# A hybrid decoder layer: thirteen shared up-projection blocks instead of ten, and more weight buffers for the feed-forward

## The chip, the cores and the metric

The kernel runs on one core of a Trainium2 chip. The metric is the device time of one execution in microseconds. A profile of one execution gives the time of each instruction on the engines: TensorE (PE, matmuls; PEld, its weight loads), VectorE (DVE), ScalarE (ACT), GpSimd (POOL), and the queue from which SyncE (SP) issues the transfers (DMA).

## What is computed

One layer on a sequence of 1024 tokens of 1024 channels, all in float32. The mixer and the feed-forward each have a norm before and after; what matters here is the feed-forward with its 2 x 2816 up columns, a causal convolution of width 3 along the tokens on each column, a gated product, and the down projection.

```python
def _conv_ffn(h, ffn_up, ffn_conv_w, ffn_conv_b, ffn_down):
    hid = h @ ffn_up.astype(h.dtype)
    hid = _causal_dwconv(hid, ffn_conv_w, ffn_conv_b)
    gate, up = hid[..., :D_FF], hid[..., D_FF:]
    return (jax.nn.gelu(gate, approximate=True) * up) @ ffn_down.astype(h.dtype)

def reference(...):
    ...
        h = _rms_norm(x, norm_pre_mix[i])
        mix, v_first = _hybrid_mixer(h, ...)
        x = x + _rms_norm(mix, norm_post_mix[i])
        h = _rms_norm(x, norm_pre_ffn[i])
        f = _conv_ffn(h, ffn_up[i], ffn_conv_w[i], ffn_conv_b[i], ffn_down[i])
        x = x + _rms_norm(f, norm_post_ffn[i])
```

The mixer before it has a recurrence over the tokens for 8 heads (in chunks of 64 tokens), a convolution of width 31 over 512 channels, and an output projection.

## The kernel before

**Products in three passes.** A float32 operand is split into a rounded part `hi` and a rest `lo` (`split`: ScalarE writes `hi`, GpSimd or VectorE subtracts to get `lo`). A product is the sum of hi x hi, hi x lo and lo x hi, three matmuls of a 128 x 128 weight with 512 tokens. A weight of 128 x 512 is loaded into a raw buffer (tag `wr`), split into a pair (tags `wh`, `wl`), and used by four input tiles, so by 12 matmuls. In the kernel before, there are 3 raw buffers and 2 pairs, in the pool `wp`.

**Tokens in two halves.** The sequence is worked on in two halves of 512 tokens, `h0` and `h1` for the feed-forward's normed input, each 8 tiles of 128 channels. The up projection has 22 blocks; block i has a gate of 128 columns and an up part of 128 columns.

**Plain blocks.** `ffn_pair(h, hs, i, ...)` computes block i for one half: two products over 8 tiles (48 matmuls), the taps of the convolution (`taps`), gelu and the product. Blocks 0 to 11 (`EARLY` = 12) are computed for the first half inside the mixer, with a low priority, so that TensorE has work while VectorE and the recurrence set the pace there; their results go to memory (`early`) and come back before the down projection. Blocks 0 to `PLAIN` - 1 = 11 are computed for the second half after the mixer, and also go to memory (`plain`).

**Shared blocks.** The last `JOINT` = 10 blocks are computed for both halves together. Gate and up columns, the two halves of the tokens, and the two halves of the 1024 channels make a product of 2 x 2 by 2 x 2 blocks; with sums of the operands it takes seven block products instead of eight (12 matmuls each). `gates` computes two of the seven with the first half alone, while the second half is normed: 24 matmuls a block, the results kept in two tiles per block of the pool `actp` (2 x `JOINT` tiles of 2 KB per partition). `act_sums` forms the sums of the activations (S), a step at a time beside the plain blocks. `shared` computes the other five: it loads the four raw weights of the block (`raws`), forms their sums on GpSimd (`four_sums`, four instructions), splits five weights, and does 60 matmuls, five additions on VectorE, and the taps of both halves. The first shared block takes sums that were formed before (`usums`).

**Side work.** `weight_sums` forms sums of down-projection weights (eleven steps, and one for the first shared block): four loads, four GpSimd instructions (L1056), four stores each. `beside` runs a step of side work between blocks: in `gates` the second half's norm first, and then norm and sums in every other block; in the plain blocks a step of sums in each, and one or two of `act_sums`.

**The down projection.** `ffn_down` is again seven products instead of eight, with 924 matmuls; it uses all 22 blocks of both halves.

**Order.** The order on each engine is set when the program is built, by a planner that simulates the engines with its own costs and takes instructions by priority as their buffers and inputs come free. `high_priority` puts loads and splits of weights ahead. All transfers are issued from SP's queue in the planned order. Buffers of a tag are reused in turn; an instruction that writes a buffer waits for the last reader.

In the mixer's end, `w_out(1, ...)`, the output projection of the second half, follows the early blocks in the same stream "proj". Its weights pass through `wr` into the buffers "ca" and "ck" of the recurrence, and its inputs are splits of `mixr` (recurrence, finished at L760) and `co` (convolution) into tiles "l8".

Of the kernel before, what the change touches and what calls it, by code (L numbers as in the profile page):

```python
# [22 lines left out]
P = 128  # L23
# [26 lines left out]
BUFS = {"v": 2, "gd": 1, "pt": 6, "kk": 1, "l8": 5, "ca": 6, "ck": 6, "r": 2,  # L50
        "mixr": 1, "co": 4, "po": 1, "c": 4, "t2": 2}

EARLY = 12

JOINT = 10
PLAIN = FT - JOINT

PRIO = {"first": -1000, "top": 100000, "rwkv": 1000, "norm": 200000, "conv": 300000, "proj": 400000}

# [39 lines left out]
class Trunk:  # L99
    def __init__(self, ctx, tc, a):  # L100
# [3 lines left out]

        self.low_pool = True


    def nm(self, s):
        self.n += 1
# [49 lines left out]
    def split(self, hi, lo, src, pool=False):  # L159

        eng = self.nc.gpsimd if pool else self.nc.vector
        return self.nc.scalar.copy(hi, src), eng.tensor_tensor(lo, src, hi.bitcast(F32), ALU.subtract)  # L162

    def weight(self, src, shape, home=None, held=None, kept=None):


        with self.tc.high_priority():
            raw = (self.f2p.tile(shape, F32, tag="f2", name=self.nm("wr")) if held is self.hp else
                   self.wp.tile(shape, F32, tag="wr", bufs=3, name=self.nm("wr")))
            self.load = self.nc.sync.dma_start(raw, src)  # L170
            if held:
                hi, lo = self.pair("w", held)
            elif home:
                hi, lo = (home[0].tile(shape, F32R, tag=t, bufs=BUFS[t], name=self.nm("wm")) for t in home[1:])
            else:
                hi, lo = (self.wp.tile(shape, F32R, tag=t, bufs=2, name=self.nm(t)) for t in ("wh", "wl"))
            if kept and kept[0]:
                self.nc.scalar.copy(hi, raw)  # L178
                self.nc.sync.dma_start(lo.bitcast(F32), kept[1])
            else:  # L180
                self.low = self.split(hi, lo, raw, self.low_pool)[1]
        if kept and not kept[0]:
            self.nc.sync.dma_start(kept[1], lo.bitcast(F32))
        return hi, lo


    def setup(self):
        nc, tc, ctx, a = self.nc, self.tc, self.ctx, self.a
        pool = lambda name, **kw: ctx.enter_context(tc.tile_pool(name=name, bufs=1, **kw))
        self.cp = pool("const")  # L190
        self.small = ctx.enter_context(tc.tile_pool(name="small", bufs=4))
        self.wp = ctx.enter_context(tc.tile_pool(name="wp", bufs=1))
        self.hp = ctx.enter_context(tc.tile_pool(name="hp", bufs=2 * KT))
        self.dp = pool("dram", space=DRAM)
        self.rowp = pool("rowp")
        self.psum = pool("psum", space=PSUM)
        cp = self.cp
        self.params = cp.tile([P, NPAR], F32, name="params")
        self.const = cp.tile([P, NCONST], F32, name="const")
        with self.stream("first"):  # L200
            nc.sync.dma_start(self.const[:, :P], a["consts"][:, :P])
        nc.sync.dma_start(self.params, a["params"])
        nc.sync.dma_start(self.const[:, P:], a["consts"][:, P:])
        self.mhalf = cp.tile([P, 8], F32, name="mhalf")
        nc.gpsimd.memset(self.mhalf, -0.5)
        self.mixd = self.dp.tile([SEQ, D], F32, name="mixd")
        self.early = self.dp.tile([EARLY, P, HALF], F32, name="early")
        self.x1d = self.dp.tile([SEQ, D], F32, name="x1d")
        self.ssq = cp.tile([P, 8, 4], F32, name="ssq")
        self.lows = self.dp.tile([22, 2, P, 4, P], F32, name="lows")  # L210
        self.sums = self.dp.tile([4, HT, P, 512], F32, name="sums")
        self.plain = self.dp.tile([PLAIN, P, HALF], F32, name="plain")
        self.usums = self.dp.tile([4, P, 512], F32, name="usums")
        self.ecarry = cp.tile([P, 2, EARLY, 2], F32, name="ecarry")

    def setup_mixer(self, ctx):
        nc, tc, a = self.nc, self.tc, self.a
        pool = lambda name, bufs=1: ctx.enter_context(tc.tile_pool(name=name, bufs=bufs))
        cp = pool("mconst")
        self.mix = pool("mix")  # L220
        self.banks = {"pb": 2, "pc": 1, "pe": 2}
        self.xs = [self.psum.tile([P, 512], F32, name=f"xs{g}") for g in range(2)]
        self.wa = cp.tile([P, HALF], F32, name="wa")

        self.dw = cp.tile([P, 16 + 1024], F32, name="dw")
        nc.gpsimd.memset(self.dw[0:64, 528:1040], 0.0)
        self.Y = self.psum.tile([P, 512], F32, name="Y")


        self.lora = cp.tile([G_LORA, D_RWKV], F32, name="lora")
        nc.sync.dma_start(self.lora, a["lora"][:G_LORA, 2])
        self.lw = cp.tile([96, 2, D_RWKV], F32R, name="lw")
        for e in range(2):
            raw = self.wp.tile([P, D_RWKV], F32, tag="wr", bufs=3, name=self.nm("wr"))
            nc.sync.dma_start(raw, a["lora"][:, e])
            nc.scalar.copy(self.lw[:, e], raw[0:96])
            low = self.lw[64:96, e]
            nc.gpsimd.tensor_tensor(low, raw[64:96], low.bitcast(F32), ALU.subtract)  # L240
        self.lx = cp.tile([96, 2, QUARTER], F32R, name="lx")
        n = POFF["k_k"]
        self.omu = cp.tile([P, n], F32, name="omu")
        nc.vector.tensor_scalar(self.omu, self.params[:, :n], -1.0, 1.0, ALU.mult, ALU.add)

        self.hw0 = cp.tile([P, 8], F32, name="hw0")
        nc.vector.tensor_scalar(self.hw0, self.params[:, POFF["w0"]:POFF["w0"] + 8], 0.5, None, ALU.mult)
        self.ka = cp.tile([P, 8], F32, name="ka")
        ka = self.params[:, POFF["k_a"]:POFF["k_a"] + 4]
        nc.vector.tensor_scalar(self.ka[:, 0:4], ka, 0.5, None, ALU.mult)  # L250
        nc.vector.tensor_scalar(self.ka[:, 4:8], ka, -0.5, 1.0, ALU.mult, ALU.add)
        cw = self.params[:, POFF["cw"]:POFF["cw"] + 4 * CONV_W]
        nc.vector.tensor_scalar(cw, cw, 0.5, None, ALU.mult)
        self.carry = cp.tile([P, n], F32, name="carry")
        self.ccarry = cp.tile([P, 4, 32], F32, name="ccarry")[:, :, :CONV_W - 1]
# [561 lines left out]
    def setup_ffn(self, ctx):  # L817
        nc, tc = self.nc, self.tc
        pool = lambda name, bufs=1: ctx.enter_context(tc.tile_pool(name=name, bufs=bufs))
        cp = pool("fconst")  # L820

        self.turn = cycle([lambda: self.xs[0], lambda: self.xs[1]]
                          + [lambda t=t: Trunk.bank(self, t) for t in ("pe", "pe", "pb", "pb")])
        self.bank = lambda tag="pb": self.Y if tag == "pn2" else Trunk.bank(self, "pc") if tag == "pn" else next(self.turn)()
        self.nrowp = pool("nrowp")

        self.ap = pool("actp", 2 * JOINT)
        self.h1p = pool("h1p", 2 * KT)
        self.tp = pool("tp", 8)
        self.f2p = pool("f2p", 6)  # L830
        self.post_ffn = cp.tile([P, D], F32, name="post_ffn")
        nc.sync.dma_start(self.post_ffn, self.a["post_ffn"].broadcast_to([P, D]))
        self.fcarry = cp.tile([P, 2, 32, 2], F32, name="fcarry")
        self.fss = cp.tile([P, 8, 48], F32, name="fss")
# [169 lines left out]
    def shared(self, i, S, A22, act0, act1, raws):  # L1004
# [10 lines left out]
        if raws is None:  # L1015
            T = lambda n: self.weight(kview(self.usums[n - 1]), [P, 4, P])
            b22 = lambda: self.weight(up[FT + i, 1], [P, 4, P])
        else:
            with self.tc.high_priority():
                b11, b12, b21, b22r = raws  # L1020
                for n in (1, 3, 0, 2):
                    self.load = nc.sync.dma_start(kview(raws[n]), up[n % 2 * FT + i, n // 2])
                t3 = self.wp.tile([P, HALF], F32, tag="wr", bufs=3, name=self.nm("t3"))
                self.four_sums(b11, b12, b21, b22r, t3)

            def pair(raw):
                with self.tc.high_priority():
                    hi, lo = (self.wp.tile([P, HALF], F32R, tag=t, bufs=2, name=self.nm(t)) for t in ("wh", "wl"))
                    self.low = self.split(hi, lo, raw, True)[1]
                return kview(hi), kview(lo)  # L1030

            T = lambda n: pair((b12, b11, t3, b21)[n - 1])
            b22 = lambda: pair(b22r)
# [167 lines left out]
    def run(self):  # L1201
# [6 lines left out]
        with ExitStack() as ctx:  # L1208
# [24 lines left out]
            for i in range(0, 8, 2):  # L1233
                two = self.row("row", 4)
                nc.sync.dma_start(two.rearrange("p (i t) -> p i t", i=2), self.early[i:i + 2].rearrange("i p t -> p i t"))
                kept += [two[:, :HALF], two[:, HALF:]]
            back = [self.hp.tile([P, HALF], F32, tag="h", name=self.nm("act")) for _ in range(2 * KT)]
            for i in range(8, EARLY):
                nc.sync.dma_start(back[PLAIN + i - 8], self.early[i])
            for i in range(PLAIN):  # L1240
# [220 lines left out]

# [6 lines left out]
```

## Time and profile before

| | |
|---|---|
| median of 3 runs | 1274.57 us (1273.83 to 1277.31) |
| profiled execution | 1273.13 us, its span 1271.4 us |
| TensorE busy | 1220.3 us (96%), 8460 matmuls |
| VectorE, ScalarE, GpSimd busy | 891.2, 731.1, 495.4 us |
| early blocks' first matmul | 497.7 us |
| second output projection, first matmul | 668.1 us |
| gates' first matmul | 698.8 us |
| plain blocks, shared blocks, down projection begin | 776.5, 911.0, 1051.9 us |

A row of the groups gives line, engine, operation, output <- inputs (buffer numbers left out), shapes and count; then busy time and mean duration in ns; then the engine's idle time before these instructions and what ended it. A row of the chain, which follows the work that ended last back to the beginning, gives start, length, engine, output and line, and the count. A row of the stages gives busy time and number of instructions of each engine in a stretch, then the granted clock of TensorE, the share of the DMA engines and GB/s. Durations of matmuls overlap. `f` are the feed-forward's inputs, `s` their sums, `wh` and `wl` a split weight; `pb`, `pe`, `pc`, `xs`, `Y` are banks of PSUM.

### The profile page before, as it was taken

To read this page: it belongs to the slowest core of one execution; us is meant where nothing else is said; L and a number is where in the kernel's file an instruction comes from. 1 tells how busy PE (TensorE), PEld (TensorE's weight loads), DVE (VectorE), ACT (ScalarE), POOL (GpSimd) and SP (SyncE) were. 2 spreads that over 40 slices of the span, in tenths; PEclk is the share of its full clock that TensorE was granted. 3 is DMA by queue.
4 is the path that set the end of the run, shared out by engine and by line. 5 is a ranking of instruction groups with operands and counts; after the bars stand their busy time and mean duration, and the time that the engine had idled before them with its cause. 6 is when DMAs were issued, how large, how long until landed. Compare 5 with 4: busy or idle time off the path is not lost.

```text
span 1271.4 us, 23025 instructions
## 1 busy us (share of the span) xinstructions
PE 1220.3 (96%) x8460; PEld 990.1 (78%) x8460; DVE 891.2 (70%) x1540; ACT 731.1 (58%) x1518; POOL 495.4 (39%) x438
## 2 busy tenths in 40 slices
PE   6999989999999988999999999999999999999996
PEld 4767767787778877788789878778877888888885
DVE  5286998998679989997631165666356779479667
ACT  7563563655845766566744277776555556545451
POOL 4343320011113332344455369898588860000001
PEclk9999998999999999999999999999999999999999
DMA  7644342343343451232345398888522236336523
GB/s 242 173 133 141 117 134 75 94 134 124 110 135 86 122 183 66 85 84 84 101 132 166 112 336 299 292 305 268 173 65 73 79 127 222 99 98 194 173 76 133
DMA packets 105505, 185.70 MB, mean 146 GB/s; under 512 B 15184, under 2 KB 21712, under 8 KB 105392
## 3 DMA queue, kind: packets, MB, share of 16 engines
q1 hardware_dynamic: 105392, 184.23, 46.2%
q8 instruction: 67, 1.10, 0.4%
q14 instruction: 46, 0.38, 0.1%
HBM read 141.58 MB, written 42.60 MB: 145 GB/s over the span
## 4 chain that ended last, share of the span: by engine, by line
PE 55%; DVE 8%; DMA 3%; POOL 3%; issue 2%; ACT 2%; SPq 0%; POOLq 0%; DVEq 0%; ACTq 0%
PE pb L135 26%; PE pe L135 13%; PE xs L135 11%; PE Y L135 2%; DVE pc L416 2%; PE pc L135 2%; POOL wl L162 1%; DVE nrow L1116 1%; DVE x L1100 1%; POOL b L1056 1%; PE pc L150 1%; DMA pt<-mixd 1%; DMA m<-mixd 1%; PE pe L150 0%; DMA b<-ffn_down 0%
## 5 line engine op out<-in xcount | busy, mean ns | idle before, releaser
L162 POOL TENSOR_TENSOR wl<-wr,wh 128x512 fp32r<-128x512 f32 (+1 forms) x181 | 237.2, 1312 | 247.7 <-ACT wh L162 221.0
L162 ACT CAST wh<-wr 128x512 fp32r<-128x512 f32 (+1 forms) x220 | 135.5, 616 | 170.7 <-issue 43.9
L135 PE MATMUL pb<-h,wh 128*128 128x512 f32 (+3 forms) x720 | 229.5, 398 | 2.5 <-ACT wh L162 1.0
L135 PE MATMUL pb<-f,wh 128*128 128x512 f32 x696 | 219.0, 395 | 2.6 <-ACT wh L162 1.5
L416 DVE SCALAR_TENSOR_TENSOR pc<-c,params,pc 128x512 f32<-128x512 f32 x232 | 174.1, 750 | 8.8 <-ACT pc L413 4.8
L135 PEld LDWEIGHTS pb<-h,wh 128*128 128x128 f32 (+2 forms) x720 | 131.8, 188 | 34.9 <-ACT wh L162 2.6
L135 PEld LDWEIGHTS pb<-f,wh 128*128 128x128 f32 x696 | 130.0, 189 | 31.0 <-ACT wh L162 2.8
L135 PE MATMUL pb<-h,wl 128*128 128x512 f32 (+3 forms) x360 | 146.4, 407 | 2.3 <-POOL wl L162 2.1
L135 PE MATMUL pb<-f,wl 128*128 128x512 f32 x348 | 137.9, 397 | 1.5 <-POOL wl L162 1.5
L157 POOL TENSOR_TENSOR ss<-var,mhalf 128x1 f32<-128x1 f32 x16 | 11.0, 692 | 222.6 <-DVE ss L1097 198.2
L1056 POOL TENSOR_TENSOR b<-b,b 128x512 f32<-128x512 f32 x66 | 86.8, 1317 | 2.8 <-issue 0.9
L135 PE MATMUL pe<-f,wh 128*128 128x512 f32 x272 | 84.2, 391 | 0.1
L135 PEld LDWEIGHTS pb<-h,wl 128*128 128x128 f32 (+2 forms) x360 | 67.7, 188 | 20.7 <-POOL wl L162 4.5
L135 PEld LDWEIGHTS pb<-f,wl 128*128 128x128 f32 x348 | 65.7, 189 | 16.9 <-POOL wl L162 3.1
L135 PE MATMUL xs<-f,wh 128*128 128x512 f32 x200 | 62.0, 391 | 0.4 <-DVE act L953 0.4
L135 PEld LDWEIGHTS pe<-f,wh 128*128 128x128 f32 x272 | 50.9, 188 | 10.6 <-ACT wh L162 0.3
L899 DVE SCALAR_TENSOR_TENSOR pt<-pb,params,pt 128x511 f32<-128x511 f32 (+1 forms) x48 | 35.7, 743 | 30.0 <-ACT ecarry L892 29.5
L162 POOL TENSOR_TENSOR wl<-b,wh 128x512 fp32r<-128x512 f32 x36 | 47.0, 1307 | 21.7 <-ACT wh L162 19.8
L135 PE MATMUL pe<-f,wl 128*128 128x512 f32 x136 | 53.7, 395 | 0.7 <-POOL wl L162 0.7
L706 POOL TENSOR_TENSOR XG<-r,GE 64x256 f32<-64x256 f32 x30 | 20.4, 683 | 86.9 <-DVE r L725 82.0
L178 ACT CAST wh<-wr 128x512 fp32r<-128x512 f32 (+2 forms) x44 | 26.5, 604 | 43.1 <-PE pb L135 31.2
L162 ACT CAST wh<-b 128x512 fp32r<-128x512 f32 x36 | 22.2, 617 | 46.8 <-PE pb L135 18.9
(428 smaller groups left out, 2883.7 us busy)
## 6 DMA issues: line engine op xcount, KB each, us to landing
wr<-ffn_up SPq DMA_DIRECT2D x117, 256.0 KB, 2.8
wr<-w_in SPq DMA_DIRECT2D x80, 256.0 KB, 2.9
b<-ffn_down SPq DMA_DIRECT2D x44, 256.0 KB, 4.4
sums<-b SPq DMA_DIRECT2D x44, 256.0 KB, 4.0
wr<-sums SPq DMA_DIRECT2D x44, 256.0 KB, 2.7
lows<-wl SPq DMA_DIRECT2D x40, 256.0 KB, 3.3
wl<-lows SPq DMA_DIRECT2D x40, 256.0 KB, 2.7
b<-ffn_up SPq DMA_DIRECT2D x40, 256.0 KB, 2.7
```

The source lines that it names most:

```text
L135: return self.nc.tensor.matmul(out, lhsT, rhs, start=start, stop=stop, skip_group_check=skip)
L150: self.nc.tensor.transpose(out, in_, self.con("ident")[:n, :n])
L157: self.nc.gpsimd.tensor_tensor(out, v[:, :n], self.mhalf[:, :n], ALU.pow)
L162: return self.nc.scalar.copy(hi, src), eng.tensor_tensor(lo, src, hi.bitcast(F32), ALU.subtract)
L178: self.nc.scalar.copy(hi, raw)
L416: nc.vector.scalar_tensor_tensor(out, c[:, j:j + HALF], w(j), acc, ALU.mult, ALU.add)
L706: nc.gpsimd.tensor_tensor(x[64:128], R[64:128, gs], w.GE[64:128, c, gs].unsqueeze(2).broadcast_to([64, 4, CH]), ALU.mult)
L899: nc.vector.scalar_tensor_tensor(acc[:, o:], ps[:, :HALF - o], w(j), acc[:, o:], ALU.mult, ALU.add)
L1056: sub = lambda o, x, y, op=ALU.subtract: self.nc.gpsimd.tensor_tensor(o, x, y, op)
L1100: nc.vector.scalar_tensor_tensor(x, f[c], s[:, 1:2], x, ALU.mult, ALU.add)
L1116: nc.vector.tensor_tensor(out, a, b, op)
```

## The change

`EARLY` becomes 9 and `JOINT` 13, so `PLAIN` becomes 9: three blocks that were plain in both halves become shared. The pool `actp` grows from 20 to 26 tiles. A new pool `wq` holds two raw buffers and one pair more; weights of the feed-forward take buffers of `wq` and `wp` in turn (`wtile`), those of the mixer stay with `wp`. The memory for DMA descriptors in SBUF is set to 1024 bytes, which frees the space. `ecarry` keeps its size. Fewer tiles are taken for the reload of early and plain results.

```diff
-EARLY = 12
-JOINT = 10
+EARLY = 9
+JOINT = 13
 PLAIN = FT - JOINT
+RAW, MORE_RAW, PAIRS, MORE_PAIRS = 3, 2, 2, 1
...
+        once = [None]
+        self.homes = {"wr": cycle(once), "wh": cycle(once), "wl": cycle(once)}
...
+    def wtile(self, tag, shape, dt=F32):
+        pool = next(self.homes[tag]) or self.wp
+        bufs = {self.wp: (RAW, PAIRS), self.wq: (MORE_RAW, MORE_PAIRS)}[pool][tag != "wr"]
+        return pool.tile(shape, dt, tag=tag, bufs=bufs, name=self.nm(tag))
...
     def weight(self, src, shape, home=None, held=None, kept=None):
...
-                   self.wp.tile(shape, F32, tag="wr", bufs=3, name=self.nm("wr")))
+                   self.wtile("wr", shape))
...
-                hi, lo = (self.wp.tile(shape, F32R, tag=t, bufs=2, name=self.nm(t)) for t in ("wh", "wl"))
+                hi, lo = (self.wtile(t, shape, F32R) for t in ("wh", "wl"))
...
+        self.wq = ctx.enter_context(tc.tile_pool(name="wq", bufs=1))
...
-        self.ecarry = cp.tile([P, 2, EARLY, 2], F32, name="ecarry")
+        self.ecarry = cp.tile([P, 2, 12, 2], F32, name="ecarry")
...
     def setup_ffn(self, ctx):
...
+        self.homes = {"wr": cycle([self.wq] * MORE_RAW + [self.wp] * RAW),
+                      **{t: cycle([self.wq] * MORE_PAIRS + [self.wp] * PAIRS) for t in ("wh", "wl")}}
...
     def shared(self, i, S, A22, act0, act1, raws):
...
-                t3 = self.wp.tile([P, HALF], F32, tag="wr", bufs=3, name=self.nm("t3"))
+                t3 = self.wtile("wr", [P, HALF])
...
-                    hi, lo = (self.wp.tile([P, HALF], F32R, tag=t, bufs=2, name=self.nm(t)) for t in ("wh", "wl"))
+                    hi, lo = (self.wtile(t, [P, HALF], F32R) for t in ("wh", "wl"))
...
-            back = [self.hp.tile([P, HALF], F32, tag="h", name=self.nm("act")) for _ in range(2 * KT)]
+            back = [self.hp.tile([P, HALF], F32, tag="h", name=self.nm("act")) for _ in range(PLAIN + EARLY - 8)]
...
-    nc = bacc.Bacc("TRN2", target_bir_lowering=False, num_devices=1)
+    nc = bacc.Bacc("TRN2", target_bir_lowering=False, num_devices=1, dynamic_dma_scratch_size=1024)
```

More of the change, by code (lines that the diff above doesn't have):

```diff
@@ L235, in setup_mixer @@
         for e in range(2):
-            raw = self.wp.tile([P, D_RWKV], F32, tag="wr", bufs=3, name=self.nm("wr"))
+            raw = self.wtile("wr", [P, D_RWKV])
             nc.sync.dma_start(raw, a["lora"][:, e])
```

## The prediction

> **What bounds the kernel now.** I read the page first (shares, slices, chain), then busy times by stage, then the chain in order of time, then what TensorE waits for in the feed-forward.
>
> ```profile
> span 1271.4 us, 23025 instructions
> PE 1220.3 (96%) x8460; PEld 990.1 (78%) x8460; DVE 891.2 (70%) x1540; ACT 731.1 (58%) x1518; POOL 495.4 (39%) x438
> PE   6999989999999988999999999999999999999996
> DVE  5286998998679989997631165666356779479667
> POOL 4343320011113332344455369898588860000001
> DMA  7644342343343451232345398888522236336523
> PE 55%; DVE 8%; DMA 3%; POOL 3%; issue 2%; ACT 2%; SPq 0%; POOLq 0%; DVEq 0%; ACTq 0%
> ```
>
> TensorE (PE) is busy 96% of the span and is the largest part of the chain; from slice 16 on it shows 9 up to the last. POOL is high in slices 23 to 32 only, DMA in slices 23 to 28 (counted from 0). So each stage behind about 500 us is as long as its matmuls, unless something feeds them late. What a matmul costs there is not its mean duration, since they overlap, but the length of an unbroken run:
>
> ```profile
> 850.57 5.44 PE pb L135 x24
> 986.16 10.90 PE pb L135 x48
> 1041.21 10.88 PE pb L135 x48
> ```
>
> 10.90 us for 48 is 0.227 us for one matmul of 512 columns. The stages:
>
> ```profile
> core 0: us, PE busy (x) PEld busy (x) DVE busy (x) ACT busy (x) POOL busy (x), PEclk, DMA share, GB/s
> 628.00:668.00 40.00, 37.95 (x166) 30.76 (x166) 15.86 (x23) 21.20 (x43) 20.56 (x16) 1.00 0.44 126
> 668.00:699.00 31.00, 31.00 (x259) 30.96 (x258) 5.61 (x7) 12.65 (x32) 16.52 (x14) 1.00 0.57 169
> 699.00:776.00 77.00, 74.70 (x396) 62.62 (x395) 35.70 (x63) 42.21 (x99) 43.32 (x36) 1.00 0.71 239
> 776.00:911.00 135.00, 133.55 (x582) 107.80 (x581) 75.03 (x111) 95.15 (x200) 110.57 (x88) 1.00 0.80 268
> 911.00:931.00 20.00, 18.35 (x77) 13.79 (x76) 10.97 (x16) 10.03 (x21) 17.32 (x14) 1.00 0.34 122
> 931.00:1052.00 121.00, 120.94 (x527) 97.52 (x526) 79.83 (x116) 67.91 (x141) 94.29 (x72) 1.00 0.33 98
> 1052.00:1060.00 8.00, 8.00 (x37) 6.63 (x36) 8.00 (x13) 4.59 (x11) 0.00 (x0) 1.00 1.05 386
> ```
>
> In order: the last early blocks; the second output projection alone; its rest with the gates of the ten shared blocks; the twelve plain blocks of the second half; the shared blocks (two rows); the first 8 us of the down projection.
>
> **The change, part by part.** A plain block costs 48 matmuls in each half. A shared block costs 24 in the gates and 60 (five products of 12) in the shared stage: 84 for both halves instead of 96. Three blocks change kind:
>
> - Early blocks in the mixer, 12 to 9: 3 x 48 = 144 matmuls fewer, 144 x 0.227 = -32.7 us.
> - Gates, 10 to 13: 3 x 24 = 72 more, +16.3 us.
> - Plain blocks of the second half, 12 to 9: 144 fewer, -32.7 us.
> - Shared stage, 10 to 13: 3 x 60 = 180 more, +40.9 us.
>
> The sum is 36 matmuls fewer, -8.2 us. With the stages' real lengths per block (135 / 12 = 11.25 us plain, 141 / 10 = 14.1 us shared, stalls and transposes included) it is -32.7 + 16.3 - 33.8 + 42.3 = -7.9 us.
>
> **Does the mixer give its 32.7 us back?** Only if those blocks are on the path there. One row of PE and two of VectorE (DVE) by time, a group of DVE from 632 to 674 us, and a row of the chain:
>
> ```profile
> 604.18 1.14 PE L135 MATMUL Y<-r,ca 128*64 128x64 f32 x16
> 622.52 0.69 DVE L760 TENSOR_TENSOR mixr<-mixr,pe 128x512 f32<-128x512 f32 x1
> 629.36 2.50 DVE L162 TENSOR_TENSOR l<-co,l 128x512 fp32r<-128x512 f32 x4 [0.56 <-ACT l L162]
> L912 DVE TENSOR_TENSOR row<-pt,pt 128x512 f32<-128x512 f32 x4 | 3.4, 856 | 0.1
> 633.05 46.72 PE pb L135 x250
> ```
>
> The mixer's own work ends with L760 at 623.2 us and the last split of the output projection's inputs at 631.9 us. After that four more early blocks end (x4), and PE runs without a break from 633.05 to the projection at 668. Three of these four blocks go. The projection then starts at 668.1 - 32.7 = 635.4 us, 3.5 us after its inputs are ready: the cover is thin but there. If the planner's order put those splits later, what is over 3.5 us would be lost. The projection's weights, also moved up by 32.7 us, need POOL for 16 splits: POOL is busy 20.56 of 40 us there, so half is free. Their buffers are those of the recurrence, which reads them last at 605.3 us (`Y<-r,ca`). I take the whole -32.7.
>
> **Other engines, per changed block.** Rows of the plain stage (776 to 911), of the shared stage (931 to 1050), and of the whole run:
>
> ```profile
> L162 POOL TENSOR_TENSOR wl<-wr,wh 128x512 fp32r<-128x512 f32 x49 | 63.3, 1293 | 21.9 <-ACT wh L162 21.4 <-DMA wr<-ffn_up 0.2 <-DMA usums<-b 0.2
> L1056 POOL TENSOR_TENSOR b<-b,b 128x512 f32<-128x512 f32 x39 | 50.5, 1294 | 1.9 <-issue 0.9
> L162 POOL TENSOR_TENSOR wl<-t,wh 128x512 fp32r<-128x512 f32 x9 | 13.5, 1505 | 1.2 <-ACT wh L162 1.2
> L1048 DVE TENSOR_TENSOR act<-act,acc 128x512 f32<-128x512 f32 x8 | 9.8, 1227 | 0.0
> L899 DVE SCALAR_TENSOR_TENSOR acc<-xs,params,acc 128x511 f32<-128x511 f32 (+1 forms) x16 | 11.2, 743 | 6.3 <-ACT fcarry L892 6.3
> L1116 DVE TENSOR_TENSOR act<-act,act 128x512 f32<-128x512 f32 x17 | 11.2, 680 | 0.0
> ```
>
> POOL does 8 splits (10.3 us) for a block that is plain twice, and 7 splits and 4 sums (14.3 us) for a shared one; DVE some 7.5 and 12 us (8 taps at 0.74, a copy, five additions and two products). So 12 us more on POOL and 14 on DVE, all in the shared stage, where PE needs 13.6 us per block, POOL 11.8 and DVE 79.83 / 121 = 66%. I cost them at nothing; PE's run covers them. ACT makes one cast fewer per block. DMA falls: two weight loads, two stores and two reloads fewer per block, 18 transfers of 256 KB in all. With them goes the work on SP's queue, and some of the burst of reloads at 1052 (386 GB/s), which stops nobody today.
>
> The plain stage gets tighter. The twelve sums of weights (eleven of the down projection, one of the up) are now spread over four side turns in thirteen gates and eight of nine plain blocks, before three and nine of twelve. A plain block with a sum takes POOL 4 x 1.293 + 4 x 1.294 = 10.4 us of the 10.9 that PE takes, and moves 13 x 262 KB = 3.4 MB, or 313 GB/s. Both hold today in nine blocks; the three blocks without a sum, in which they could catch up, shrink to one.
>
> **The buffers.** Raw weight buffers of the feed-forward go from 3 to 5, split pairs from 2 to 3. What they can win is bounded by PE's waits from 690 to 1050 us:
>
> ```profile
> PE pb L135 <- POOL wl L162: 1.0, 2, 0.7
> PE pb L135 <- ACT wh L162: 0.8, 2, 0.5
> PE pe L135 <- ACT wh L162: 0.8, 1, 0.8
> PE pe L135 <- POOL wl L162: 0.7, 1, 0.7
> PE xs L135 <- POOL wl L162: 0.7, 2, 0.3
> PE pc L150 <- ACT nrow L872: 0.4, 1, 0.4
> ```
>
> The five rows on weights (`wh`, `wl`) sum to 4.0 us; that is the most there is. A pair is 12 matmuls, 2.7 us of lookahead; a sum's four POOL instructions take 5.2, so a third pair should hide about half: I take -1.5 us, between 0 and -4. Against it stands the tighter plain stage: bounded by nothing, and by 8 blocks x 1 us (a block with a sum at 11.9 instead of 10.9), +8 us; I take 0, since the present nine such blocks cost less than the 4.0 us above. The smaller descriptor memory: the trace has one queue with data, filled from SP (q1, hardware_dynamic, below), and no transfer issued by POOL; I take nothing. The first feed-forward loads now have free buffers from the beginning, and could be issued far earlier, at worst among the loads of the first slices: two of 262 KB at the first slice's 242 GB/s are 2.2 us; I take 0, as the planner follows priorities.
>
> ```profile
> q1 hardware_dynamic: 105392, 184.23, 46.2%
> ```
>
> [...]
>
> From the rows alone: a shared block loses 1.23 - 0.68 = 0.55 us on DVE, which has slack.
>
> **The sum.** The profiled execution took 1273.1 us, 1.7 over its span: 1273.1 - 8.2 - 1.5 = 1263.4. It is 1.4 below the median of the three runs, 1274.57; against that median it is 1264.9. I say 1264.5.
>
> **Rivals.**
>
> 1. POOL or DMA sets the pace of the plain stage (or POOL of the shared one: 11.8 us plus one blocked stretch of 1.2 is 13.0 of 13.6). For it: slices of POOL at 9 and 8, the 1505 ns of `wl<-t`. Against it: PE waited 4.0 us in all. Price up to +8, all of the gain: 1270 to 1274. Chance 0.13.
> 2. The mixer does not shorten: the output projection starts when something else than the early blocks lets it, a bank, a weight or a planner's order that puts the splits late. If it did not move at all, the feed-forward's +24.5 us would remain: 1298. It decides from 10 us on: a projection that starts at 645 instead of 635 us eats the gain, and behind 649 the kernel is slower by over 0.3%. Against it: inputs ready at 631.9 and POOL half idle. Chance 0.06.
> 3. The deeper buffers and the longer gates, which also cover the second norm (0.4 us on `nrow`), remove every stall: PE's idle time in the four rows from 699 to 1052 us is 2.3 + 1.5 + 1.7 + 0.1 = 5.5 us, 4.0 more than I took: 1261. Chance 0.16.
> 4. The buffers do nothing, but the matmuls go: 1266.4. This lies within the forecast's own case.
>
> **How the numbers follow.** The forecast (1262 to 1268, its own range) has 0.65, rival 3 0.16, rival 1 0.13, rival 2 0.06. The three runs span 0.27%, so 0.3%, 3.8 us, is about what can be told from no change: faster is below 1270.7. The forecast, rival 3 and a small part of rival 1 give 0.83; the rest of rival 1 and a part of rival 2 give 0.11 the same; 0.06 slower. The range 1259.5 to 1270 leaves out most of rivals 1 and 2.
>
> **What would show it.** 8424 matmuls instead of 8460. Early blocks ending near 639 us and the projection starting at 635 to 637. Gates and their neighbours 16 us longer than 77, plain stage near 100 us, shared stage near 182. PE's waits on `wh` and `wl` behind 690 us at 1 to 4 us in all. The down projection starting 8 to 10 us earlier than 1052 and as long as before. Wrong would be: idle PE before the projection (rival 2), or a plain stage of more than 103 us with waits for POOL or `wr` (rival 1).

## The result, and the profile after

| | before | after |
|---|---|---|
| median on one chip, 6 runs each | 1274.61 us (1273.53 to 1277.31) | 1265.88 us (1262.7 to 1266.88) |
| ratio | | 0.992 [0.9906, 0.9935] |
| profiled execution, its span | 1273.13, 1271.4 us | 1266.88, 1265.1 us |
| early blocks' first matmul | 497.7 us | 513.8 us |
| second output projection, first matmul | 668.1 us | 647.9 us |
| from there to the end of the span | 603.3 us | 617.2 us |

The forecast was 1264.5 us, and the time is 1265.88. The two parts of which it was made are not: the projection starts 20.2 us earlier, where 32.7 were forecast, and what follows takes 13.9 us longer (617.2 for 603.3), where 24.5 - 1.5 = 23.0 were. Two errors of 12.5 and 9.1 us nearly cancel; that the sum came out so close is luck. The experiments below are about these two.

The page of the kernel after, span, engines, TensorE's slices and the chain's shares:

```profile
span 1265.1 us, 22976 instructions
PE 1216.0 (96%) x8424; PEld 993.7 (79%) x8424; DVE 901.4 (71%) x1558; ACT 730.6 (58%) x1516; POOL 512.2 (40%) x447
PE   5999999999998998999999999999999999999997
PE 78%; DVE 10%; ACT 5%; issue 2%; DMA 2%; POOL 2%; SPq 0%; POOLq 0%; DVEq 0%; ACTq 0%
```

8424 matmuls, as counted. The chain's share of PE has gone from 55 to 78%; this alone says little, since the fastest kernels below have 62%. The stages after, as in the prediction (busy time of each engine with its instructions, granted clock, DMA share, GB/s), with two starts from TensorE's rows by time:

```profile
513.78 0.89 PE L139 MATMUL pb<-f,wh 128*128 128x512 f32 x2 [0.23 <-DVE sub L602]
514.00:648.00 134.00, 133.80 (x1245) 107.35 (x1246) 108.06 (x175) 83.61 (x173) 60.78 (x50) 1.00 0.31 90
647.93 2.31 PE L139 MATMUL pb<-wm,l 128*128 128x256 f32 x18
675.00:771.00 96.00, 95.30 (x516) 81.89 (x516) 41.40 (x74) 51.27 (x117) 58.35 (x50) 1.00 0.71 249
771.00:869.00 98.00, 98.00 (x434) 81.16 (x433) 61.09 (x91) 75.06 (x157) 87.36 (x70) 1.00 0.88 290
869.00:889.00 20.00, 20.00 (x89) 16.44 (x89) 12.29 (x18) 11.32 (x24) 19.19 (x15) 1.00 0.38 128
889.00:1044.00 155.00, 155.00 (x685) 128.34 (x685) 105.32 (x154) 88.30 (x184) 126.42 (x97) 1.00 0.31 92
```

The plain stage (771 to 869) and the shared one (869 on, shown to 1044) have no idle PE at all: 98.00 of 98, 20.00 of 20, 155.00 of 155. POOL works 87.36 of the plain stage's 98 us and is still never late. All that PE waits for between 668 and 1044 us is this, and none of it is a weight:

```profile
PE pb L139 <- ACT pb L799: 0.4, 1, 0.4
PE xs L139 <- DVE act L966: 0.3, 1, 0.3
```

So the feed-forward came out better than forecast. What came out worse lies ahead of the early blocks: they start 16.1 us later than before, in the mixer, whose work the change does not touch.

### The profile page after: what moved, and what is told of

Read it like the earlier page. It is cut to its first block, busy times and chain, and to the rows that moved or that the text cites. A ratio compares the mean times of both kernels' runs of the same rounds, so it can differ in the third digit from the quotient of the medians.

```text
span 1265.1 us, 22976 instructions
## 1 busy us (share of the span) xinstructions
PE 1216.0 (96%) x8424; PEld 993.7 (79%) x8424; DVE 901.4 (71%) x1558; ACT 730.6 (58%) x1516; POOL 512.2 (40%) x447
## 4 chain that ended last, share of the span: by engine, by line
PE 78%; DVE 10%; ACT 5%; issue 2%; DMA 2%; POOL 2%; SPq 0%; POOLq 0%; DVEq 0%; ACTq 0%
PE pb L139 39%; PE xs L139 17%; PE pe L139 16%; DVE pc L427 3%; PE Y L139 2%; PE pc L139 2%; POOL wl L166 1%; PE pe L154 1%; DVE dw L604 1%; DMA pt<-mixd 1%; DMA params<-params 1%; DVE pt L496 1%; PE pc L154 1%; DVE sub L602 1%; PE xs L154 0%
## 5 line engine op out<-in xcount | busy, mean ns | idle before, releaser
L166 POOL TENSOR_TENSOR wl<-wr,wh 128x512 fp32r<-128x512 f32 (+2 forms) x175 | 233.7, 1337 | 226.0 <-ACT wh L166 188.9
L139 PE MATMUL pb<-f,wh 128*128 128x512 f32 x648 | 203.2, 393 | 0.7 <-ACT pb L799 0.4
L139 PEld LDWEIGHTS pb<-f,wh 128*128 128x128 f32 x648 | 120.9, 188 | 26.1 <-issue 1.0
L139 PE MATMUL pb<-f,wl 128*128 128x512 f32 x324 | 128.0, 396 | 0.0
L139 PE MATMUL xs<-f,wh 128*128 128x512 f32 x240 | 74.1, 390 | 0.3 <-DVE act L966 0.3
L166 POOL TENSOR_TENSOR wl<-b,wh 128x512 fp32r<-128x512 f32 x48 | 67.1, 1398 | 13.4 <-ACT wh L166 11.6
L139 PE MATMUL pe<-f,wh 128*128 128x512 f32 x208 | 64.1, 389 | 0.0
L139 PEld LDWEIGHTS xs<-f,wh 128*128 128x128 f32 x240 | 44.9, 188 | 9.9 <-DVE act L966 0.8
L166 ACT CAST a<-act 128x512 fp32r<-128x512 f32 x50 | 30.0, 619 | 33.4 <-PE Y L139 18.9
L166 ACT CAST w<-wr 128x512 fp32r<-128x512 f32 x38 | 23.5, 622 | 41.3 <-PE Y L139 20.0
```

Source lines behind the costliest of these rows:

```text
L139: return self.nc.tensor.matmul(out, lhsT, rhs, start=start, stop=stop, skip_group_check=skip)
```

## The experiments

### The two halves of the change, each alone

Without the buffers: 13 shared blocks and 9 early ones, all weights in `wp`.

```diff
     def setup_ffn(self, ctx):
-        self.homes = {"wr": cycle([self.wq] * MORE_RAW + [self.wp] * RAW), ...}
```

> This kernel has the 13 shared and 9 early blocks, but no weight buffer beyond those of the kernel before. Theory A (the extra buffers disturb the mixer: their first two loads wait for nothing, are queued at the very beginning, and the planned order of the mixer comes out another way; the early blocks then start 16 us later, the output projection at 647.9 instead of 635.4): without those buffers the mixer runs as before, early blocks from 497 to 499 us, projection at 635 to 637 us; PE's stalls in the plain and shared stages stay near those before (134.3 us for 12 plain blocks, 140.7 for 10 shared, against 130.6 and 136.0 at full rate). Total 1265 us, 0.992 to 0.995 of before. Theory B (the mixer loses because three early blocks fewer leave VectorE and the recurrence without cover): projection at 645 to 649 us here too, and with the stalls 1274 to 1278 us, ratio 1.000 to 1.004.

1271.42 us (1267.71 to 1273.64), 0.9972 [0.9958, 0.9987]. Starts of the early blocks and of the projection, then the plain and the shared stage:

```profile
498.07 0.70 PE L139 MATMUL pb<-f,wh 128*128 128x512 f32 x2 [0.61 <-DVE f L290]
634.81 2.44 PE L139 MATMUL pb<-wm,l 128*128 128x256 f32 x19
761.00:865.00 104.00, 100.29 (x433) 80.14 (x432) 60.72 (x90) 74.85 (x157) 89.72 (x71) 1.00 0.85 284
865.00:885.00 20.00, 18.68 (x79) 14.07 (x78) 12.27 (x18) 11.05 (x23) 17.04 (x14) 1.00 0.43 151
885.00:1049.00 164.00, 163.19 (x706) 131.01 (x707) 103.76 (x156) 90.26 (x188) 130.49 (x99) 1.00 0.31 91
```

Here the mixer is where it was (498.1 us), and the projection starts at 634.8, 33.3 us earlier: the early blocks' step, 635.4, is right when nothing else moves. But the plain stage takes 104 us for 98 us of matmuls. From the projection's start to the end of the span it is 1268.7 - 634.8 = 633.9 us, 30.6 more than before instead of 24.5: with the old buffers, three more shared blocks cost 6 us of new stalls. The mixer does what theory A says; its time of 1265 us is missed, because it took the stalls as near those of before.

Without the blocks: the buffers with `EARLY` 12 and `JOINT` 10.

```diff
-EARLY = 9
-JOINT = 13
+EARLY = 12
+JOINT = 10
```

> This kernel has the 10 shared and 12 early blocks of before, with the extra weight buffers and the smaller descriptor memory. Theory A: the mixer is late as in the changed kernel, early blocks from 510 to 514 us and the projection 10 to 16 us later than 668; plain and shared stages lose their stalls (about -8 us together). Total 1276 to 1282 us, ratio 1.002 to 1.006. Theory B: the mixer runs as before, the stalls go: 1264 to 1267 us, ratio 0.993 to 0.995.

1275.92 us (1272.22 to 1278.11), 1.0015 [1.0001, 1.0029]. The projection's start and the plain stage:

```profile
678.28 1.96 PE L139 MATMUL pb<-wm,l 128*128 128x256 f32 x15
783.00:915.00 132.00, 131.68 (x583) 108.20 (x583) 76.72 (x116) 95.83 (x204) 111.77 (x89) 1.00 0.84 277
```

This is theory A (0.1 us below its range). The buffers alone win nothing, and this zero is two large numbers: the projection is 10.2 us later than before, and from there to the end it takes 1270.3 - 678.3 = 592.0 instead of 603.3 us, 11.3 less. So the late mixer belongs to the buffers, not to the blocks. How can buffers of the feed-forward delay a mixer that never uses them? SP's DMA issues by time in the first microseconds (start, length, output <- input, count), after, and below it before:

```profile
1.19 3.74 SPq L302 DMA_DIRECT2D l<-x  x8
4.97 1.18 SPq L180 DMA_DIRECT2D wr<-ffn_up  x2
6.20 0.65 SPq L213 DMA_DIRECT2D params<-params  x1
```

```profile
1.19 3.75 SPq L291 DMA_DIRECT2D l<-x  x8
4.98 0.80 SPq L202 DMA_DIRECT2D params<-params  x1
```

Nobody has read the two new raw buffers, so they are free at 0 us, and the planner issues the first two loads of the feed-forward (needed behind 497 us) right behind the first eight tiles of `x`, ahead of the mixer's `params`, which go out 1.2 us later than before.

### Holding those two loads back

The order on SP alone is changed: the first two loads into `wq` are planned behind a given load of the mixer, in e3 the last load of the early blocks, in e3b the last one of the second output projection. No wait is added, and the buffers stay.

```diff
     def weight(...):
-        with self.tc.high_priority():
+        with ExitStack() as gate, self.tc.high_priority():
+            if self.fresh:
+                self.fresh -= 1
+                gate.enter_context(self.tc.issue_after(self.held_behind.ins))
...
     def setup_ffn(self, ctx):
+        self.fresh = MORE_RAW
...
+        self.held_behind = self.load        # e3: behind the early blocks; e3b: behind w_out(1)
```

> This is the changed kernel, but the two loads that are the first to use the new raw buffers are queued on SP behind the last weight load of the early blocks. Theory A: the mixer runs as before (early blocks from 497 to 499 us, projection at 635 to 638 us) and the feed-forward without stalls as in the changed kernel: 1273.1 - 8.2 - 8 = 1257 us, between 1254 and 1260, ratio 0.985 to 0.989 of before. Theory B: nothing moves against the changed kernel, projection at 645 to 649 us, 1264 to 1267 us, ratio 0.991 to 0.994.

> As the kernel with held first loads, but they are queued behind the last weight load of the second output projection, some 25 us later. Theory A: the mixer as before, projection at 635 to 637 us; the first gates get their weights later, so 0 to 3 us slower than with the earlier place: 1255 to 1262 us, ratio 0.986 to 0.991. Theory B: as the changed kernel, 1264 to 1267 us.

e3: 1252.87 us (1252.57 to 1253.87), 0.9828 [0.9805, 0.9852]. e3b: 1252.68 (1251.63 to 1255.63), 0.9829 [0.9804, 0.9854]. Two starts and two stages of e3:

```profile
497.28 0.70 PE L140 MATMUL pb<-f,wh 128*128 128x512 f32 x2 [0.62 <-DVE f L294]
634.88 2.33 PE L140 MATMUL pb<-wm,l 128*128 128x256 f32 x17
757.00:855.00 98.00, 98.00 (x434) 81.16 (x433) 60.55 (x90) 75.13 (x158) 86.84 (x69) 1.00 0.88 293
875.00:1030.00 155.00, 155.00 (x686) 128.27 (x685) 103.68 (x156) 87.91 (x184) 126.04 (x96) 1.00 0.32 92
```

The mixer is back at 497.3 us, the projection at 634.9, and the feed-forward is as unbroken as after. The mixer of both does what theory A says, and both are faster than its ranges (1254 to 1260 and 1255 to 1262 us). e3 beats the kernels before and after, by 1.7% and by about 13 us. Against e1, the same blocks without the buffers, it is 1271.42 - 1252.87 = 18.5 us faster: that is what the buffers are worth once the two loads are held.

### What the early loads cost: their transfers, their cast and subtraction, or the order?

e4 keeps both loads held and adds one load of 256 KB that nothing reads, behind the mixer's own first loads. The planner then finds nearly the order of the kernel after (35 of the first 3000 entries on PE differ from it, 648 from before).

```diff
             self.load_rows(1, rows)
+            for i in range(1):
+                nc.sync.dma_start(self.wq.tile([P, 512], F32, tag="wr", bufs=MORE_RAW, ...), self.a["ffn_up"][i, 0])
```

> The kernel with held first loads, and one added load of 256 KB that nothing reads, queued behind the mixer's own first loads (place 15 of SP's queue). With it the planner orders TensorE's mixer nearly as in the changed kernel (35 of the first 3000 entries differ; 648 differ from before). Theory A (the planned order is what costs; the work done early costs nothing): the beginning is not delayed, but early blocks start at 507 to 515 us and the whole takes 1262 to 1269 us, 10 to 16 us more than with held loads (1252.9). Rival C (what costs is the early work itself, two loads, a cast and a subtraction among the first loads, delaying the beginning): early blocks at 497 to 499 us, 1252 to 1255 us.

1261.62 us (1261.23 to 1262.68), 0.9902 [0.9889, 0.9915]: 8.75 us slower than e3 (on another chip, where before took 1274.38 us and not 1273.63), and 0.4 below theory A's range. Its early blocks start at 506.9 us, 9.6 late, and its projection at 641.5, 6.6 late. At 389 us it is only 0.2 us behind e3 (table below), so the added transfer itself is not what costs: the order is. Of the early loads, e8 lets the first go early, with its cast and its subtraction, and holds the second (`if not self.fresh:` ahead of the gate).

> The changed kernel with only the second of the two first loads held: the first one, its cast and its subtraction are done at the very beginning, as in the changed kernel; the mixer's planned order is that of the changed kernel but for 31 of the first 3000 entries of TensorE. Theory A (order): early blocks at 506 to 514 us, 1261 to 1267 us. Rival C (the amount of early work): with about half of it about half of the loss, early blocks at 500 to 505 us, 1255 to 1260 us.

1260.09 us (1259.2 to 1261.66), 0.9889 [0.987, 0.9909], early blocks at 506.7: theory A's start, and a time 0.9 us below its range. One real load with its work costs what the dummy costs: the work of one load is not it. e9 is e4 with two dummies (`range(2)`), which gives a third order.

> The kernel with held first loads and two added loads that nothing reads, queued behind the mixer's own first loads. The planner then makes a third order of the mixer (486 of the first 3000 entries differ from before, 349 from the changed kernel). Theory A: the loss is a property of the order, so it is not tied to the number of loads: early blocks anywhere from 490 to 515 us, with VectorE's wait for TensorE at the evacuation of the first output projection (6.2 us in the changed kernel) present if they are late, absent if they are at 500 or earlier. Rival C: two loads cost more than one (which gave 506.9 us): 508 to 516 us.

1259.33 us (1256.68 to 1260.32), 0.9879 [0.9858, 0.9899]. Its early blocks start at 500.6, only 3.3 us late, but the convolution's last splits come 10 us later than in e3 and the projection starts at 637.4. A changed order is thus not always a loss of the same size, nor at the same place. The kernel after once more, beside these:

> The changed kernel as it is, on the same chip as the two before it: 1263 to 1267 us, early blocks at 510 to 514 us, projection at 645 to 648 us.

1265.48 us (1261.19 to 1266.77), 0.9921 [0.9892, 0.9949], early blocks at 512.8.

The traces show the orders themselves. Up to the first matmul of the early blocks, before, e1, e3 and e3b (and e6 and e7 below) execute the same order on PE and VectorE, and these blocks start from 496.3 to 498.1 us in all six. After, its repeat (e10) and e2 share another order, and that of e4 and e8 is nearly this one (150 and 148 of 4316 places on PE differ from after, 1276 between e4 and before). Three marks, in us:

| | before | e3 | e4 | e8 | e9 | e2 | e10 | after |
|---|---|---|---|---|---|---|---|---|
| first `kk<-pe` on VectorE | 41.13 | 40.55 | 41.38 | 41.73 | 42.82 | 42.21 | 43.20 | 44.02 |
| `gd<-carry` on VectorE | 389.07 | 389.28 | 389.47 | 389.00 | 389.83 | 391.15 | 391.99 | 393.02 |
| early blocks' first matmul | 497.65 | 497.28 | 506.92 | 506.73 | 500.60 | 509.95 | 512.80 | 513.78 |

So the loss has two parts. With both loads early (e2, e10, after) the mixer is already 1.9 to 3.7 us behind e3 at 389 us, and this begins in the first 44 us; with one early load or with dummies it is at most 0.6 us. These three kernels also share their order, so that the two loads alone cause it is likely, not shown. The larger part, 9.4 to 12.8 us in the five late kernels, comes behind 389 us.

How the order costs is seen from 390 to 520 us. The same stretch of e3, e4 and after:

```profile
390.00:520.00 130.00, 121.80 (x1644) 105.79 (x1644) 121.66 (x236) 83.93 (x193) 41.94 (x41) 0.98 0.37 113
```

```profile
390.00:520.00 130.00, 114.62 (x1483) 98.89 (x1481) 112.60 (x225) 79.67 (x185) 40.90 (x38) 0.97 0.36 108
```

```profile
390.00:520.00 130.00, 114.59 (x1351) 99.17 (x1349) 109.71 (x224) 77.68 (x182) 40.06 (x36) 0.93 0.35 106
```

VectorE is the mixer's pace: 121.66 of 130 us busy in e3. In e4 it does 9 us less in the same time, after 12. What it waits for, after, is in VectorE's rows by time (in brackets the idle time before the instruction and what ended it), and below it two of the same evacuations of the first output projection in e3:

```profile
409.94 0.69 DVE L793 TENSOR_TENSOR t<-pb,po 128x512 f32<-128x512 f32 x1 [3.15 <-PE pb L139]
469.88 0.69 DVE L793 TENSOR_TENSOR t<-pb,po 128x512 f32<-128x512 f32 x1 [2.39 <-PE pb L139]
471.20 0.69 DVE L793 TENSOR_TENSOR t<-pb,po 128x512 f32<-128x512 f32 x1 [0.62 <-PE pb L139]
```

```profile
403.49 0.68 DVE L797 TENSOR_TENSOR t<-pb,po 128x512 f32<-128x512 f32 x1
456.13 0.68 DVE L797 TENSOR_TENSOR t<-pb,po 128x512 f32<-128x512 f32 x1
```

The sums of these waits from 388 to 475 us (total, times, longest), after, in e4 and in e8; before, e3 and e9 have no such row:

```profile
DVE t L793 <- PE pb L139: 6.2, 3, 3.1
```

```profile
DVE t L797 <- PE pb L140: 4.9, 3, 2.6
```

```profile
DVE t L797 <- PE pb L140: 6.4, 3, 3.1
```

Around the first of these waits VectorE's own order is the same as in e3; it is PE that comes late, and VectorE starts nothing in the 3.15 us ahead of `t<-pb,po`. PE has waited 2.15 us for a split weight, since POOL's subtraction for it took 4.89 us. It takes 4.89 or 4.90 us in e2, e4, e8 and e10 too, and 3.26 in e9; in before and e3 no subtraction of POOL from 394 to 415 us takes more than 1.90. The long one runs beside five subtractions of VectorE that split the projection's inputs (398.9 to 402.8 us, with two other instructions between them); whether these hold POOL up, no run tests. POOL and PE after, then the same subtraction of POOL in e3:

```profile
399.01 4.89 POOL L166 TENSOR_TENSOR wl<-wr,wh 128x512 fp32r<-128x512 f32 x1 [6.15 <-ACT wh L166]
403.95 0.51 PE L139 MATMUL pb<-wl,m 128*128 128x256 f32 x2 [2.15 <-POOL wl L166]
```

```profile
396.44 1.76 POOL L167 TENSOR_TENSOR wl<-wr,wh 128x512 fp32r<-128x512 f32 x1 [8.52 <-ACT wh L167]
```

PE then serves VectorE at a lower clock. Stretches of 5 us, after, in which the third number from the end is the clock, and PE's rows with idle time between 445 and 450 us:

```profile
400.00:405.00 5.00, 2.85 (x24) 2.65 (x23) 5.00 (x10) 0.62 (x1) 5.00 (x2) 0.99 0.00 0
405.00:410.00 5.00, 5.00 (x32) 5.00 (x31) 1.85 (x6) 0.62 (x1) 1.12 (x2) 0.66 0.38 105
445.00:450.00 5.00, 2.14 (x49) 1.62 (x49) 4.96 (x9) 4.84 (x13) 2.49 (x3) 0.93 0.74 189
450.00:455.00 5.00, 5.00 (x24) 4.93 (x24) 4.85 (x8) 1.90 (x8) 0.00 (x0) 0.50 0.76 214
```

```profile
447.17 0.34 PE L139 MATMUL xs<-r,l 128*64 128x64 f32 x4 [1.10 <-ACT l L662]
448.18 0.57 PE L139 MATMUL xs<-r,l 128*64 128x64 f32 x12 [0.68 <-ACT l L662]
449.69 0.58 PE L139 MATMUL pe<-lx,lw 96*128 96x256 f32 x1 [0.94 <-ACT l L658]
```

PE works 2.85 and 2.14 us of 5, and in the next 5 us its granted clock is 0.66 and 0.50; in the first of these VectorE works 1.85 us. Matmuls of 256 columns then start every 0.21 us (13 from 405.05 to 407.83 us, 22 from 450.45 to 455.15), at a granted clock of 1.00 every 0.12 (20 from 408.54 to 410.94); by these rates the low clock costs PE 1.2 and 2.1 us there, an estimate. The idle time ahead of the lower of the two, 0.50, is 2.9 us in 5, in pieces of 1.10, 0.68 and 0.94 us with small matmuls between. Not every such pause is followed by a low clock: from 70 to 75 us PE works 2.95 of 5 us in before and 2.94 in e3, and the clock of the next 5 us is 0.70 in before and 1.00 in e3. What lowers the clock, no run tests.

The waits named are 5 to 6 us; e4 lost 9.6 and after 16.5 against e3. Of the 7 us between these two, 3.6 are there at 389 us. What is left behind 389 us, 9.4 and 9.7 us in e4 and e8, 10.8 in e2, 12.8 after and in e10, goes with the mean clock of this stretch (0.97, 0.96, 0.96, 0.93, 0.92), and e2 has the order of after. No run separates the clock's share from the order's own, so the reason for these last 2 to 3 us stays open.

### Which of the buffers

On e3, the pair of split weights alone (`MORE_RAW` 0, `MORE_PAIRS` 1), and the two raw buffers alone (2 and 0), the first load held in the first, the first two in the second.

> The kernel with held first loads, but with the extra pair alone (3 raw buffers, 3 pairs). The buffers together are worth 1271.4 - 1252.9 = 18.5 us at 13 and 9 blocks. If the pair is what hides POOL's sums (theory P): plain stage within 1 us of 97.9, shared stage within 2 of 176.8, 1253 to 1257 us. If raw buffers are what was short, since a raw buffer is held from the issue of its load to the end of its subtraction (theory W): 1264 to 1271 us.

> The kernel with held first loads, but with the two extra raw buffers alone (5 raw buffers, 2 pairs). Theory P: stalls as without any extra buffer, 1265 to 1271 us, plain stage 102 to 104 us. Theory W: 1253 to 1258 us, plain stage within 1 us of 97.9.

The pair alone: 1257.32 us (1255.09 to 1257.7), 0.9863 [0.9849, 0.9877], 14.1 of the 18.5 us. The raw buffers alone: 1264.77 (1263.85 to 1267.88), 0.9933 [0.9919, 0.9947], 6.6 of them. The mixer is in place in both (projection at 634.8 and 635.1 us). The stages, in us, each from its first matmul to that of the next, the shared stage to the end of its last matmul:

| | projection and gates | plain | shared | rest |
|---|---|---|---|---|
| e1, no buffer more | 126.7 | 104.1 | 183.6 | 219.4 |
| e7, raw buffers | 123.8 | 99.8 | 183.3 | 220.0 |
| e6, pair | 125.5 | 98.1 | 179.0 | 217.9 |
| e3, both | 122.1 | 97.9 | 178.4 | 217.9 |

The pair does in the plain and the shared stage what theory P says, and its time is 0.3 us above P's range. The raw buffers help mostly ahead of the plain stage and in it, and their time and plain stage lie between the two theories. The lookahead that counts most here is PE's over POOL and ACT (`wh`, `wl`; 14.1 us), not that over the DMA (6.6 us).

### One block less ahead of the projection

`EARLY` 8 on e3, with one tile more in `actp`.

> The kernel with held first loads, but 8 early blocks: block 8 of the first half is computed behind the mixer (one tile more in actp). Theory A with the margin as traced (inputs of the projection ready at 633.2, projection at 634.9 us with 9 early blocks): the projection can move up by 1 to 3 us only, PE idles some 8 to 10 us ahead of it, and the block's 48 matmuls come on top behind it: 1260 to 1264 us, 8 to 11 us slower than 1252.9. Rival D (the inputs come earlier when VectorE has a block less): projection at 624 to 628 us, 1252 to 1256 us.

1256.43 us (1256.13 to 1259.78), 0.9866 [0.985, 0.9881], 3.6 us slower than e3. The projection starts at 623.8 us, 11.1 earlier, where rival D had it, but ahead of it, from 619.6 us on, PE waits 3 us, and the granted clock is 0.83 from 620 to 640 us. PE's longest wait from 610 to 690 us, and the stretch:

```profile
PE pc L155 <- DVE t L447: 3.0, 1, 3.0
620.00:640.00 20.00, 17.05 (x116) 16.33 (x117) 12.82 (x17) 12.98 (x28) 9.13 (x7) 0.83 0.43 141
```

The plain stage starts only 6.8 us earlier than in e3 (750.2 for 757.0 us), and the block taken away puts its 48 matmuls into it, 10.9 us more (108.8 for 97.9). The time lies between what the theories expected, 0.4 us above D's range. The cover was thin, as the prediction says, and nine blocks use nearly all of it.

## Why the prediction was right in its sum and wrong in two terms

- **36 matmuls fewer, -8.2 us.** Right: 8424, and the plain and shared stages run at 0.227 us for each matmul.
- **The early blocks, -32.7 us.** Right as a step: -33.3 in e1, -33.2 in e3.
- **"The first feed-forward loads now have free buffers from the beginning ... I take 0, as the planner follows priorities."** This step failed. They are issued at 4.97 us, as its worst case had it; but their price is not only the 2.2 us of their bytes. The mixer's `params` go out 1.2 us later, its work is 3.7 us behind at 389 us, and its planned order changes; all together cost 13.0 us at the projection (647.9 against 634.9 in e3); the order alone cost 6.6 there (e4). Rival 2 came about in part (its loss begins at 645), by another way than it had in mind: the splits of the projection's inputs are late indeed (the last ends at 653.0 us, 631.9 before), but PE shows no idle time ahead of the projection (133.80 of 134 us from 514 to 648), which begins when the early blocks end. What is late are the early blocks, from their start on. A transfer was costed alone, though the prediction's own account of the order, set when the program is built, means that it can move everything behind it.
- **The buffers, "the most there is" 4.0 us, taken as -1.5.** The term was mis-sized: 11.3 us with the old blocks (e2), 18.5 with the new (e3 against e1). The bound was read from PE's waits, and these are counted from the shown ends, which lie behind the next starts: a matmul of 512 columns is shown as 0.39 us long, and in an unbroken run the next starts 0.227 behind it, so that a late one has little idle time before it. The prediction had a better bound and did not use it: the plain and the shared stage took 135 and 141 us for 576 and 600 matmuls, which at 0.227 are 130.8 and 136.2, together 9 us of stalls, in these two stages alone. In e2 these two gave 6.2 of the 11.3 us, the projection with the gates 3.6 and the rest 1.5.
- **Rival 3, every stall gone.** Right in kind, and too small for the same reason: it had 5.5 us.
- **Rival 1, a tight plain stage.** True without the buffers (e1: 104 us, over its sign of 103), and removed by them. The prediction weighed the two as separate terms, 0 and -1.5; they are one, as the buffers cover what the denser sums ask. The 1.2 us for which it has POOL blocked in the shared stage is the mean length of L1048; POOL's instruction beside L1048 takes 1.73 to 1.80 us in seven of eight blocks of before, 0.4 to 0.5 more than its usual 1.29.
- **Other engines at nothing, the smaller descriptor memory at nothing.** POOL's splits take longer in the shared stage (1402 ns, 1293 in the plain stage before), and VectorE's products too (1012 ns; 680 for L1116, of the same shape, in before, where POOL is idle), here from 889 to 1044 us after:

```profile
L166 POOL TENSOR_TENSOR wl<-b,wh 128x512 fp32r<-128x512 f32 x46 | 64.5, 1402 | 13.4 <-ACT wh L166 11.6 <-PE pb L139 1.7
L1061 DVE TENSOR_TENSOR act<-act,acc 128x512 f32<-128x512 f32 x11 | 11.1, 1012 | 0.0
```

  PE's two waits above show that neither delays it. The smaller descriptor memory is in e1 too, and its mixer runs as before (498.1 us).

Of the signs listed, matmuls, plain stage (97.9 us, forecast near 100), shared stage (177.7, near 182) and gates (96.2 for 77.7 us, 16 longer forecast) came, roughly; the early blocks and the projection did not, and PE's waits on `wh` and `wl` are 0 instead of 1 to 4. The down projection starts at 1043.6 us, 8.3 earlier as forecast, but by the same two errors that cancel. With the two terms as measured, the sum for the profiled execution is: -33.3 for the early blocks, +30.6 for the blocks behind (e1), -16.7 for the buffers (633.9 to 617.2), +13.1 for the mixer (634.8 to 647.9); together -6.3, the spans' difference.

## What to carry to other kernels

A buffer that nobody has used is free from the first microsecond. Where a planner sets the order, the loads into it can go to the very front and reorder work that has nothing to do with them (here at 4.97 us, for 13.0 us at the projection); look at the first issues of the queue, and tie such loads to the place where they are wanted. Size stalls of TensorE by a stage's length less its matmuls at the rate of an unbroken run (here 9 us in two stages), not by the waits that the profile shows before them (4.0 us).

## What was not expected of the hardware

Twice in the kernel after, a stretch of 5 us in which PE pauses for 2 to 3 us in all is followed by a stretch at a granted clock of 0.66 and 0.50 (405 to 410 and 450 to 455 us), in which matmuls of 256 columns start every 0.21 us instead of 0.12 and in the first of which VectorE waits 3.15 us for PE. One subtraction of POOL, at most 1.9 us long in before and e3, takes 4.9 us in all five late kernels, after beside five subtractions of VectorE. And of 11.3 us that the deeper buffers gave at ten shared blocks (e2), the profile of before showed 4.0 as waits for weights.
